# Recurrence's inverse: diagonal blocks gathered and scattered by ScalarE, transposed 64 rows at a time

## The chip, the cores and the metric

One core of a Trainium2 chip runs the whole program. The metric is the device time of one execution in microseconds; lower is better. The engines are called PE (TensorE's matmuls; PEld its weight loads), DVE (VectorE), ACT (ScalarE), POOL (GpSimd) and SP (SyncE, which issues most of the DMAs).

## What is computed

The reference is a trunk of two layers over 256 tokens of 1024 channels, in float32. In each layer three branches (latent attention with 8 heads, a spatial-gating MLP, a bidirectional RWKV-7 recurrence with 8 heads of 64) start from the same normed input, are merged by gates, and a SwiGLU follows. The part that matters here is the recurrence:

```
def step(st, inp):
    r_t, w_t, k_t, v_t, kk_t, b_t = inp
    sa = jnp.einsum('dbhij,dbhj->dbhi', st, kk_t)
    st = (st * w_t[..., None, :] - sa[..., :, None] * b_t[..., None, :]
          + v_t[..., :, None] * k_t[..., None, :])
    return st, jnp.einsum('dbhij,dbhj->dbhi', st, r_t)
```

The kernel computes it in 4 chunks of 64 tokens, for 2 directions and 8 heads: 64 systems of 64 unknowns each, whose triangular matrices have to be inverted.

## The kernel before, in words

**The threads.** The mixer of each layer is built by three generators (`interleave`): `products` (weight products for the gates, the spatial gating, the branches), `attention` and `recurrent`. Each yields the cost of what it has issued, divided by its speed (1.0, 0.5, 1.1); the thread that is behind goes next. This gives the order in which the program is written down. From it the framework's planner fixes the queue of each engine before the program runs, with costs and dependences of its own; it may put an instruction ahead of an earlier one that is not ready in its reckoning. On the chip each queue runs strictly in order.

**Weights.** A weight group arrives by DMA, ACT makes its rounded half (L347), DVE the remainder (L348), and PE uses both (L368, L380). Three to seven slots hold them, and an ACT cast waits until PE has released its slot. So every weight passes through ACT and DVE, in the same queues as the recurrence's small work.

**Recurrence.** `rw_prep` ends for each of four channel tiles with products of 64 x 64 blocks (L878) that DVE masks and writes to `MM` (L881), and PE transpositions (L884) that ACT copies out (L885). PSUM tiles of these come from a pool of two. `rw_inverse` then inverts. `MM` is laid out as [128 partitions, direction d, 32 systems u, 128 columns]: partitions 0 to 63 serve direction 0, 64 to 127 direction 1, and columns 0 to 63 hold the triangular matrix. Its 32 x 32 diagonal blocks are found at quarter q of the partitions (32 rows), d = q // 2, b = q % 2, columns 32b to 32b + 31.

- Gather (L901 to L906): for each q one DVE transposition of 32 x 1024 takes the blocks of all 32 systems out of `MM` into `Lb`, so that each of the 128 partitions then holds one system's block. It reads runs that lie 128 columns apart and changes the order of the loops on the way.
- Elimination (L907 to L914): 31 steps of two DVE operations (L910, L912) over `Lb` and `X`, which ends as the inverse of the blocks.
- L918 and L919: two transpositions of 32 x 1024 into `DN`, a copy of two of the inverted blocks in the form that the next products want.
- Scatter (L920 to L924): for each q, in the order 1, 2, 0, 3, one DVE transposition of 32 x 1024 back into `MM`.
- Two rounds of products of 32 x 32 blocks on PE put the off-diagonal blocks together. The first (L933, L934) reads `DN` and `MM`; its PSUM tiles are copied to `Wt` by ACT (L935, rows 32 to 63) and DVE (L936, rows 64 to 95). The second (L944, L945) reads `Wt` and the diagonal blocks 1 and 2 in `MM`, writes the two PSUM tiles of the same pool, and is copied to `MM` by L946 and L947.

**Attention** meets it on PE, DVE and ACT: L581 and L583 bring queries and keys into transposed form, L597 makes scores, L600 (DVE) their maxima, L603 (ACT) the exponentials, L611, L613 and L616 the transposition and the product with the values. The buffer that L583 writes shares memory with one that L884 reads.

**Memory.** `Wt` lies on columns that `rw_prep` has used for temporaries and that nothing holds between the end of `rw_prep` and L917.

Of the kernel before, what the change touches and what calls it, by code (L numbers as in the profile page):

```python
# [60 lines left out]
CI, CC, CA = 1.2, 0.8, 1.2  # L61
# [153 lines left out]
def v3(ap, b):  # L215
    return ap.rearrange("p (a b) -> p a b", b=b)
# [37 lines left out]
def trunk(ctx: ExitStack, tc: tile.TileContext, x_in, pos, wts, vecs, rows, lora, sgw, consts, out):  # L254
    nc = tc.nc
# [13 lines left out]
    ph = Phase()  # L269
# [13 lines left out]
    def pr(name="r"):  # L283
        return ps_r.tile([P, 512], F32, tag="r", name=name)
# [606 lines left out]
    def rw_inverse(MM):  # L891

        Lb = ph.get("Lb")
        X = ph.get("X")
        pt = ph.get("prod")
        nc.gpsimd.memset(X, 0.0)
        nc.gpsimd.memset(X[:, 0:1024:33], -1.0)
        MMu = MM.rearrange("p d a b c t -> p d (a b c) t")
        L3, X3 = v3(Lb, 32), v3(X, 32)
        for q in range(4):  # L900
            d, b = q // 2, q % 2  # L901
            qs = slice(32 * q, 32 * q + 32)
            src = MMu[qs, d, :, 32 * b:32 * b + 32].rearrange("p u t -> p t u")
            dst = L3[qs] if d == 0 else L3[qs].rearrange("p s t -> p t s")
            nc.vector.transpose(dst, src)  # L905
            yield 1.2 * CI  # L906
        for c in range(31):  # L907
            n, m = 31 - c, c + 1
            t = v3(pt[:, :n * m], m)
            TT(t, L3[:, c + 1:32, c:c + 1].broadcast_to([P, n, m]),  # L910
               X3[:, c:c + 1, 0:m].broadcast_to([P, n, m]), ALU.mult)
            TT(X3[:, c + 1:32, 0:m], X3[:, c + 1:32, 0:m], t, ALU.subtract)  # L912
            if c % 4 == 3:
                yield 2.0 * CI  # L914
        ph.put("prod", "Lb")
        DN = v3(ph.get("DN"), 32)
        Wt = v3(ph.get("Wt"), 32)  # L917
        nc.vector.transpose(DN[0:32].rearrange("p u s -> p s u"), X3[0:32].rearrange("p t s -> p s t"))  # L918
        nc.vector.transpose(DN[96:128].rearrange("p u s -> p s u"), X3[96:128])  # L919
        for q in (1, 2, 0, 3):  # L920
            d, b = q // 2, q % 2
            qs = slice(32 * q, 32 * q + 32)
            src = X3[qs] if d == 0 else X3[qs].rearrange("p s t -> p t s")
            nc.vector.transpose(MMu[qs, d, :, 32 * b:32 * b + 32].rearrange("p u t -> p t u"), src)  # L924
        ph.put("X")
        yield 5.0 * CI
        for hb in range(2):
            ps = pr()
            us = slice(16 * hb, 16 * hb + 16)
            for j in range(16):  # L930
                u = 16 * hb + j
                o = slice(j * 32, (j + 1) * 32)
                mm(ps[32:64, o], lhsT=MMu[0:32, 0, u, 32:64], rhs=DN[0:32, u, :], start=True, stop=True)  # L933
                mm(ps[64:96, o], lhsT=MMu[96:128, 1, u, 0:32], rhs=DN[96:128, u, :], start=True, stop=True)  # L934
            nc.scalar.copy(Wt[32:64, us, :], v3(ps[32:64, :], 32))  # L935
            nc.vector.tensor_copy(Wt[64:96, us, :], v3(ps[64:96, :], 32))  # L936
            yield 2.0 * CI
        for hb in range(2):
            ps = pr()
            us = slice(16 * hb, 16 * hb + 16)  # L940
            for j in range(16):
                u = 16 * hb + j
                o = slice(j * 32, (j + 1) * 32)
                mm(ps[0:32, o], lhsT=Wt[32:64, u, :], rhs=MMu[32:64, 0, u, 32:64], start=True, stop=True)  # L944
                mm(ps[96:128, o], lhsT=Wt[64:96, u, :], rhs=MMu[64:96, 1, u, 0:32], start=True, stop=True)  # L945
            nc.scalar.copy(MMu[0:32, 0, us, 32:64], v3(ps[0:32, :], 32))  # L946
            nc.vector.tensor_copy(MMu[96:128, 1, us, 0:32], v3(ps[96:128, :], 32))  # L947
            yield 2.0 * CI
        ph.put("DN", "Wt")
# [251 lines left out]
    for l in range(L):  # L1201
# [34 lines left out]
        def recurrent():  # L1236
            def blocks(*bs):
                while not all(("z", b) in done for b in bs):
                    yield None

            yield from blocks(12, 13, 4, 5, 6, 7)
            g2g = ph.get("g2g").rearrange("p (i c) -> p i c", i=2)
            ect = ph.get("ect").rearrange("p (n d c) -> p n d c", n=4, d=2)
            bon = ph.get("bon").rearrange("p (i h) -> p i h", i=2)
            MM = ph.at(*MIX["MM"][0]).rearrange("p (d a b c t) -> p d a b c t", d=2, a=4, b=2, c=4)
            vtok = yield from rw_prep(l, z, blocks, lo, ARF, BK, MM, ect, bon, g2g)
            done.add("p")
            yield from rw_inverse(MM)
            while "a" not in done:
                yield None  # L1250
            yield from rw_chain(l, vtok, ARF, BK, MM, ect, bon, g2g, yTc)
# [180 lines left out]
```

## Time and profile before

| | us |
|---|---|
| median of 3 runs | 1056.88 (1055.81 to 1060.32) |
| the profiled execution, its own time | 1058.36 |
| its span from first to last instruction | 1056.6 |
| busy in it: PE | 1026.2 |
| busy in it: DVE | 748.0 |
| busy in it: ACT | 548.8 |

The profile is one execution. Busy times are sums over the engine's instructions; matmuls are pipelined, and their ends are modelled, so a busy PE need not be at its peak. PEclk, or the clock, is the TensorE clock that the chip granted, as a share of full speed (2.4 GHz); 0.50 is 1.2 GHz. A "wait" is idle time of an engine, with what released it. Line numbers are those of the kernel before.

### The profile page before, as it was taken

To read this page: it belongs to the slowest core of one execution; us is meant where nothing else is said; L and a number is where in the kernel's file an instruction comes from. 1 tells how busy PE (TensorE), PEld (TensorE's weight loads), DVE (VectorE), ACT (ScalarE), POOL (GpSimd) and SP (SyncE) were. 2 spreads that over 40 slices of the span, in tenths; PEclk is the share of its full clock that TensorE was granted. 3 is DMA by queue.
4 is the path that set the end of the run, shared out by engine and by line. 5 is a ranking of instruction groups with operands and counts; after the bars stand their busy time and mean duration, and the time that the engine had idled before them with its cause. 6 is when DMAs were issued, how large, how long until landed. Compare 5 with 4: busy or idle time off the path is not lost.

```text
span 1056.6 us, 21287 instructions
## 1 busy us (share of the span) xinstructions
PE 1026.2 (97%) x8810; PEld 925.5 (88%) x8810; DVE 748.0 (71%) x1247; ACT 548.8 (52%) x903; POOL 42.0 (4%) x60
## 2 busy tenths in 40 slices
PE   9999999989999999999999999999999999999997
PEld 7987788988898899998899868889889978999885
DVE  5786899995757856664467869999857676666543
ACT  5756674644445544443366565655434465444431
POOL 2010000000200000000011000000001000000000
PEclk8999999999999999999999999999999999999999
DMA  7533441413356765653655333324215567555531
GB/s 267 190 117 101 128 143 68 140 62 112 137 180 232 274 195 187 181 181 96 208 211 185 118 109 104 122 81 140 97 48 203 200 211 264 191 186 180 180 140 40
DMA packets 46050, 164.06 MB, mean 155 GB/s; under 512 B 5233, under 2 KB 5761, under 8 KB 45954
## 3 DMA queue, kind: packets, MB, share of 16 engines
q1 hardware_dynamic: 43346, 153.90, 42.8%
q0 software_dynamic: 2464, 8.54, 2.4%
q8 instruction: 69, 1.13, 0.4%
q14 instruction: 27, 0.22, 0.1%
q10 hardware_dynamic: 144, 0.26, 0.1%
HBM read 160.59 MB, written 2.10 MB: 154 GB/s over the span
## 4 chain that ended last, share of the span: by engine, by line
PE 77%; DVE 11%; issue 4%; ACT 4%; POOL 1%; DMA 1%; SPq 0%; DVEq 0%; POOLq 0%; ACTq 0%
PE g L368 41%; PE g L380 22%; DVE permr L348 2%; DVE mix L924 1%; PE r L878 1%; PE m L616 1%; DMA permf<-in_wts_dram 1%; DVE mix L905 1%; PE m L597 1%; PE r L1036 1%; ACT mix L771 1%; PE r L815 1%; POOL yrs L409 1%; PE r L979 1%; DVE mix L824 1%
## 5 line engine op out<-in xcount | busy, mean ns | idle before, releaser
L368 PE MATMUL g<-permr 128*128 128x256 f32 x3168 | 421.3, 289 | 0.0
L368 PEld LDWEIGHTS g<-permr 128*128 128x128 f32 x3168 | 393.5, 193 | 6.4 <-issue 2.2
L348 DVE TENSOR_TENSOR permr<-permf,permr 128x1024 fp32r<-128x1024 f32 (+4 forms) x179 | 213.6, 1195 | 83.0 <-ACT permr L347 80.2
L347 ACT CAST permr<-permf 128x1024 fp32r<-128x1024 f32 (+4 forms) x179 | 183.0, 1025 | 147.0 <-PE g L368 96.5
L380 PE MATMUL g<-permr 128*128 128x512 f32 (+2 forms) x804 | 181.3, 376 | 0.0
L380 PEld LDWEIGHTS g<-permr 128*128 128x128 f32 x804 | 142.7, 190 | 24.0 <-issue 3.9
L368 PE MATMUL g<-permr,more 128*128 128x256 f32 x1008 | 121.1, 281 | 0.0
L368 PEld LDWEIGHTS g<-permr,more 128*128 128x128 f32 x1008 | 119.4, 189 | 0.0
L348 DVE TENSOR_TENSOR more<-permf,more 128x1024 fp32r<-128x1024 f32 x48 | 58.8, 1225 | 36.1 <-ACT more L347 36.0
L380 PE MATMUL g<-more,permr 128*128 128x512 f32 x324 | 79.2, 395 | 0.0
L348 DVE TENSOR_TENSOR more<-raw,more 128x1024 fp32r<-128x1024 f32 x38 | 46.5, 1225 | 43.8 <-ACT more L347 43.8
L347 ACT CAST more<-permf 128x1024 fp32r<-128x1024 f32 x48 | 50.1, 1047 | 48.7 <-PE g L368 32.5
L380 PEld LDWEIGHTS g<-more,permr 128*128 128x128 f32 x324 | 60.3, 188 | 13.7 <-DVE more L348 0.7
L347 ACT CAST more<-raw 128x1024 fp32r<-128x1024 f32 x38 | 40.0, 1051 | 51.1 <-PE g L368 23.9
L380 PE MATMUL g<-more,aT 128*128 128x512 f32 x192 | 45.5, 391 | 0.0
L380 PEld LDWEIGHTS g<-more,aT 128*128 128x128 f32 x192 | 36.0, 188 | 7.6
L348 DVE TENSOR_TENSOR permr<-raw,permr 128x1024 fp32r<-128x1024 f32 x22 | 26.9, 1224 | 21.6 <-ACT permr L347 21.6
L347 ACT CAST permr<-raw 128x1024 fp32r<-128x1024 f32 x22 | 23.0, 1044 | 26.2 <-PE g L368 12.0
L297 ACT ACTIVATE permr<-m 128x512 fp32r<-128x512 f32 (+2 forms) x36 | 19.6, 563 | 20.3 <-PE m L436 16.4
L878 PE MATMUL r<-mix,mix 64*64 64x128 f32 x512 | 28.0, 276 | 0.0
L414 ACT ACTIVATE ffn<-ffn 128x512 f32<-128x512 f32 x16 | 10.1, 630 | 33.3 <-DVE ffn L1137 33.3
L878 PEld LDWEIGHTS r<-mix,mix 64*64 64x64 f32 x512 | 21.8, 132 | 6.3 <-issue 2.9
(268 smaller groups left out, 1183.6 us busy)
## 6 DMA issues: line engine op xcount, KB each, us to landing
permf<-in_wts_dram SPq DMA_DIRECT2D x210, 512.0 KB, 4.3
raw<-in_wts_dram SPq DMA_DIRECT2D x60, 512.0 KB, 4.3
permf<-in_wts_dram SPq DMA_DIRECT2D x6, 504.0 KB, 4.8
mix<-in_rows_dram POOLq DMA_DIRECT2D x8, 256.0 KB, 3.8
ffn<-in_rows_dram POOLq DMA_DIRECT2D x4, 512.0 KB, 5.7
mix<-in_lora_dram SPq DMA_DIRECT2D x2, 768.0 KB, 7.3
permf<-in_wts_dram SPq DMA_DIRECT2D x4, 384.0 KB, 3.6
mix<-in_sgw_dram SPq DMA_DIRECT2D x2, 512.0 KB, 4.8
```

Of the source, the lines that this page charges most:

```text
L297: a = act(hi, src, AF.Copy, scale=scale)
L347: nc.scalar.copy(hi, raw)
L348: TT(lo, raw, hi.bitcast(F32), ALU.subtract)
L368: newest[0] = mm(ps, lhsT=wt[:, k, c:c + 128], rhs=xt[:, k, :], start=n == 0, stop=n == 3 * kt - 1).ins
L380: newest[0] = mm(pss[i][:, :n], lhsT=xt[:, k0 + k, i * 128:(i + 1) * 128], rhs=wt[:, k, :], start=k0 + k + q == 0, stop=q == 2 and k0 + k ...
L409: powers[:] = [nc.gpsimd.tensor_tensor(dst, src, mhalf[:, :n], ALU.pow).ins]
L597: mm(ps[:, b * 256:(b + 1) * 256], lhsT=qT[0:96, h, b * 128:(b + 1) * 128], rhs=kT[0:96, h, :], start=True, stop=True)
L616: mm(pso[:, b * 256 + h * 64:b * 256 + (h + 1) * 64], lhsT=v3(pts, 128)[:, kt * 2 + b, :], rhs=vt[:, kt, h, :], start=kt == 0, stop=kt == 1)
L771: nc.scalar.copy(dst[q * 64:(q + 1) * 64, i, :], ps[hf * 64:(hf + 1) * 64, :])
L815: mm(psd[d][hf * 64:(hf + 1) * 64, q * 256:(q + 1) * 256], lhsT=w[ds_, co:co + 64], rhs=z[ds_, 12 + q, :], start=True, stop=True)
L824: nc.vector.tensor_tensor_scan(inc, rmult, lw, 0.0, ALU.mult, ALU.add)
L878: mm(psh[hp][o, c * 128:(c + 1) * 128], lhsT=xf[hs, 4 * d + c, o], rhs=A8[hs, 4 * d + c, :], start=True, stop=True)
```

## The change

The gather is done in two steps: ACT copies the diagonal blocks of each quarter (32 rows) from `MM` into a contiguous buffer with the order of the two loops exchanged (the buffer is `Wt`, taken early and given back), and DVE transposes both quarters of a direction in one instruction of 64 rows. The scatter is done the same way backwards: one DVE transposition of 64 rows per direction into `Wt`, then two ACT copies of 32 rows into `MM`. The order of the quarters in the scatter becomes 0, 1, 2, 3. Each half of the gather yields a cost of 2.0 where each of its four quarters yielded 1.2.

```diff
--- before.py
+++ after.py
@@ -897,13 +897,16 @@
         nc.gpsimd.memset(X[:, 0:1024:33], -1.0)
         MMu = MM.rearrange("p d a b c t -> p d (a b c) t")
         L3, X3 = v3(Lb, 32), v3(X, 32)
-        for q in range(4):
-            d, b = q // 2, q % 2
-            qs = slice(32 * q, 32 * q + 32)
-            src = MMu[qs, d, :, 32 * b:32 * b + 32].rearrange("p u t -> p t u")
-            dst = L3[qs] if d == 0 else L3[qs].rearrange("p s t -> p t s")
-            nc.vector.transpose(dst, src)
-            yield 1.2 * CI
+
+        B3 = v3(ph.get("Wt"), 32)
+        for d in range(2):
+            for b in range(2):
+                qs = slice(64 * d + 32 * b, 64 * d + 32 * b + 32)
+                nc.scalar.copy(B3[qs].rearrange("p t u -> p u t"), MMu[qs, d, :, 32 * b:32 * b + 32])
+            ds = slice(64 * d, 64 * d + 64)
+            nc.vector.transpose(L3[ds] if d == 0 else L3[ds].rearrange("p s t -> p t s"), B3[ds])
+            yield 2.0 * CI
+        ph.put("Wt")
         for c in range(31):
             n, m = 31 - c, c + 1
             t = v3(pt[:, :n * m], m)
@@ -917,11 +920,12 @@
         Wt = v3(ph.get("Wt"), 32)
         nc.vector.transpose(DN[0:32].rearrange("p u s -> p s u"), X3[0:32].rearrange("p t s -> p s t"))
         nc.vector.transpose(DN[96:128].rearrange("p u s -> p s u"), X3[96:128])
-        for q in (1, 2, 0, 3):
-            d, b = q // 2, q % 2
-            qs = slice(32 * q, 32 * q + 32)
-            src = X3[qs] if d == 0 else X3[qs].rearrange("p s t -> p t s")
-            nc.vector.transpose(MMu[qs, d, :, 32 * b:32 * b + 32].rearrange("p u t -> p t u"), src)
+        for d in range(2):
+            ds = slice(64 * d, 64 * d + 64)
+            nc.vector.transpose(Wt[ds], X3[ds] if d == 0 else X3[ds].rearrange("p s t -> p t s"))
+            for b in range(2):
+                qs = slice(64 * d + 32 * b, 64 * d + 32 * b + 32)
+                nc.scalar.copy(MMu[qs, d, :, 32 * b:32 * b + 32], Wt[qs].rearrange("p t u -> p u t"))
         ph.put("X")
         yield 5.0 * CI
         for hb in range(2):
```

## Rows read from the trace of the kernel before

**Rows 1.** The page's first part: engine, busy us, share of the span, instructions.

```profile
PE 1026.2 (97%) x8810; PEld 925.5 (88%) x8810; DVE 748.0 (71%) x1247; ACT 548.8 (52%) x903; POOL 42.0 (4%) x60
```

**Rows 2.** 10-us stretches: busy us (instructions) of each engine, clock, DMA share, GB/s.

```profile
160.00:170.00 10.00, 8.88 (x92) 7.57 (x88) 9.91 (x9) 3.08 (x6) 0.00 (x0) 1.00 0.23 74
170.00:180.00 10.00, 8.95 (x67) 8.24 (x67) 9.58 (x22) 5.83 (x20) 0.00 (x0) 1.00 0.29 105
...
220.00:230.00 10.00, 7.68 (x196) 7.30 (x196) 9.90 (x7) 3.25 (x4) 1.12 (x2) 1.00 0.17 54
230.00:240.00 10.00, 10.00 (x210) 9.27 (x204) 9.81 (x15) 4.16 (x7) 0.00 (x0) 0.83 0.15 52
...
580.00:590.00 10.00, 10.00 (x72) 8.71 (x65) 9.63 (x25) 7.34 (x15) 0.00 (x0) 0.85 0.35 120
```

**Rows 3.** What TensorE waited for: us in total, times, longest us.

```profile
PE r L944 <- DVE mix L936: 4.5, 2, 2.3
...
PE m L611 <- ACT mix L603: 2.9, 2, 1.5
...
PE r L933 <- DVE mix L918: 2.0, 2, 1.0
PE r L884 <- DVE mix L881: 1.4, 2, 0.7
```

**Rows 4.** VectorE's groups by shape: busy us, mean ns of one, idle before.

```profile
L905 DVE STREAM_TRANSPOSE mix<-mix 32x1024 f32<-32x1024 f32 x8 | 16.2, 2020 | 0.2
L924 DVE STREAM_TRANSPOSE mix<-mix 32x1024 f32<-32x1024 f32 x8 | 15.8, 1980 | 0.1
...
L1038 DVE COPY mix<-r 64x512 f32<-64x512 f32 x8 | 5.6, 695 | 9.1 <-ACT mix L1037 9.0
...
L936 DVE COPY mix<-r 32x512 f32<-32x512 f32 x4 | 2.6, 683 | 0.1
```

**Rows 5.** The same view, 150 to 260 us: work over 1024 columns.

```profile
L348 DVE TENSOR_TENSOR permr<-permf,permr 128x1024 fp32r<-128x1024 f32 x17 | 20.8, 1222 | 1.0 <-ACT permr L347 0.8
L347 ACT CAST permr<-permf 128x1024 fp32r<-128x1024 f32 x17 | 17.8, 1049 | 12.7 <-PE g L368 11.3 <-PE g L380 1.1 <-DMA permf<-in_wts_dram 0.2
```

**Rows 6.** VectorE in order of time: start us, us, what; L912's first and last step.

```profile
174.68 0.21 DVE L912 TENSOR_TENSOR mix<-mix 128x31 f32<-128x31 f32 x1
...
216.37 0.19 DVE L912 TENSOR_TENSOR mix<-mix 128x31 f32<-128x31 f32 x1
```

**Rows 7.** All engines in order of time, the gather of the first layer.

```profile
161.85 1.10 PE L878 MATMUL r<-mix,mix 64*64 64x128 f32 x32
162.42 1.97 DVE L905 STREAM_TRANSPOSE mix<-mix 32x1024 f32<-32x1024 f32 x1
...
164.32 1.23 DVE L881 TENSOR_TENSOR mix<-r,permf 128x512 f32<-128x512 f32 x2
...
165.59 4.05 DVE L905 STREAM_TRANSPOSE mix<-mix 32x1024 f32<-32x1024 f32 x2
165.60 0.60 ACT L583 ACTIVATE mix<-m 96x512 f32<-96x512 f32 x1 [3.80 <-PE r L884]
...
167.34 1.03 PE L597 MATMUL m<-mix 96*128 96x256 f32 x4
...
169.67 1.29 DVE L600 TENSOR_REDUCE nm<-m 128x2 f32<-128x512 f32 x2
```

**Rows 8.** The same, the scatter of the first layer.

```profile
220.77 7.96 DVE L924 STREAM_TRANSPOSE mix<-mix 32x1024 f32<-32x1024 f32 x4
...
222.03 0.58 ACT L935 COPY mix<-r 32x512 f32<-32x512 f32 x1 [2.81 <-PE r L934]
...
223.18 4.08 PE L368 MATMUL g<-permr 128*128 128x256 f32 x32
...
229.50 0.21 PE L944 MATMUL r<-mix,mix 32*32 32x32 f32 x1 [2.25 <-DVE mix L936]
```

**Rows 9.** 1-us stretches after the scatter, columns as in rows 2.

```profile
232.00:233.00 1.00, 1.00 (x7) 1.00 (x6) 0.96 (x2) 0.84 (x2) 0.00 (x0) 0.50 0.00 0
```

## Prediction, made before the change was run

> **What bounds the kernel now.** I read the busy shares first: TensorE is busy 97% of a span of 1056.6 us, VectorE 71% [rows 1]. A change that gives TensorE no work and takes none can only win where TensorE stands still or runs below full speed, so the next view was the span in stretches of 10 us. Nearly all of them have TensorE busy for 9.4 to 10.0 us. The two stages that this change touches do not: around the gather (160 to 180 us) it is busy 8.88 and 8.95, around the scatter (220 to 230 us) 7.68, and VectorE is at 9.6 to 9.9 in all three [rows 2]. After the scatter the granted clock averages 0.83.
>
> Which wait ends last there is in the list of what TensorE waited for. Four entries, each twice (once per layer), belong to this code: L944 waits for VectorE's L936 (4.5 us in all), L611 for ScalarE's L603 (2.9), L933 for L918 (2.0), L884 for L881 (1.4) [rows 3]. Per layer that is 2.25 + 1.45 + 1.0 + 0.7 = 5.4 us; it is the prize, beside what the clock loses. VectorE's time itself is not.
>
> **What goes and what comes.** Per layer the edit takes eight transpositions of 32 rows at 2.0 us each (L905, L924: 2.02 and 1.98) and puts four of 64 rows in their place [rows 4]. A 64-row one stands nowhere in the trace. A copy of 512 columns takes 0.683 us with 32 rows and 0.695 with 64 [rows 4], so rows cost nothing on this engine, and I take 2.0. Ends: 4.0 if the two blocks of 32 were done one after the other; 1.22, the time of a tensor operation over 1024 columns [rows 5], where the new one reads and writes unbroken runs, which none of the old ones did on both sides. VectorE so loses 4 x 2.0 = 8 us per layer, 16 in all.
>
> ScalarE gets eight copies of 32 x 1024 per layer. Nearest row: its cast of 128 x 1024, 1.05 us [rows 5]. So 8.4 us per layer, 16.8 in all. ScalarE is busy 3.1 and 5.8 us of the two 10-us stretches at the gather and 3.25 of that at the scatter [rows 2]: the time is there, the order is the question. Each copy has one side with a stride of 32 elements. What a stride costs shows only in small: L912's first call of a layer walks down a column of 31 elements with that stride, its last one along 31 neighbours, and they take 0.21 and 0.19 us [rows 6]. That is 0.02 us over 31 elements, at most 0.7 us over 1024. So 1.05 is the low end, 1.05 + 0.7 = 1.75 the high one, and I take 1.05, since a rounding step of the view is half of the difference. The Trainium skill speaks against the change here: by Advanced Engine Details and Errata, section Memory Cachelines, SBUF serves lines of 16 bytes and an access that needs a new line each time pays; no figure is given. It is a rival below, priced from the rows.
>
> **Gather, per layer.** Now the first transposition (162.42 to 164.39) stands ahead of two L881 whose products TensorE finished at 162.95; they start at 164.32, and L884 waits 0.7 us for them. Then two transpositions in a row (165.59 to 169.64) stand ahead of L600, whose scores were done near 168.4; L603 and L611 wait behind it [rows 7]. After the change the first transposition waits for two copies, 2.1 us, so it can hardly start before 164. L881 then goes ahead of it, from 162.95, and L884 and L583 come up to 1.3 us earlier. The second transposition waits for two more copies and ends near 164.2 + 2.1 + 2.0 = 168.3, so L600 starts near 168.4 instead of 169.67. Gain: 0.7 + 1.3 = 2.0 us of TensorE's idle time. Against it: the second pair of copies and the two L583 (0.60 us each) [rows 7] want ScalarE at the same time. If the copies are put first, L583, on which L597, L600, L603 and L611 hang, is 2.1 us later, against 1.3 us of advance: a loss of 0.8. L583 waits for L884, and L884 for the first of the two L881; the copies wait for both L881. So the two are ready within some 0.1 us of each other, and I take the case between, one copy ahead of L583 and one behind: 2.0 - 1.05, some 0.9.
>
> The shorter yields of the gather (4.8 cost units where there were 5.76) bring the recurrence ahead of the other threads by under one unit. I price that at nothing: TensorE's queue at 180 to 210 us is full either way. If that cover fails, it is a shift of the kind that the second rival holds.
>
> **Scatter, per layer.** Now VectorE does L918, L919 and the four L924 without a break, the four from 220.77 to 228.73; L936 follows, and L944 needs the PSUM buffer that L936 empties. TensorE's last filler ends at 227.26, L944 starts at 229.50 [rows 8]. After the change: transpositions 220.77 to 222.8 and to 224.8. ScalarE's copies begin at 222.85; four by 1.05 end at 227.05. L936 overwrites rows that the third copy reads, so it waits until 226.0 and ends at 226.7. L935, on ScalarE behind the copies, ends at 227.6 (its row: 0.58 us; it now starts at 222.03 and is long done). L944 then starts at 227.65, and the idle time is 0.4 instead of 2.25: gain 1.85. So the scatter's limit moves from VectorE to ScalarE, and only 1.85 of the 4 us that VectorE saves arrive. ScalarE's casts of weights in these microseconds slip by 2 to 3 us; VectorE's backlog, busy 9.81 us of the next 10 [rows 2], stands ahead of their other halves and hides that. Without it the slip would reach TensorE. Ends: 2.25 (all of the wait) and -1.0 (copies at 1.75: 222.85 + 7.0 + 0.6 = 230.45 against 229.5).
>
> L933's wait of 1.0 us hangs on L918, the end of the chain of 31 steps, which has L348 between its steps; I book nothing, between 0 and 1.0.
>
> **Clock.** At 232 us the granted clock stands at 0.50 (1.2 GHz) with TensorE busy all the time [rows 9]. A mean of 0.83 over 10 us [rows 2] is 3.4 us at that level, 1.7 us of work lost, per layer. It has fallen by 2.5 us after the idle time before L944. If that goes, the fall may go; but the stretch 580 to 590 has a mean of 0.85 with TensorE busy for all 10 us [rows 2], so idle time is not the only thing that brings one. I book half, 0.85, between 0 and 1.7.
>
> **Sum.** Per layer 0.9 + 1.85 + 0.85 = 3.6, twice 7.2 us. The profiled execution took 1058.36 us, 1.76 more than its span, and lies 1.5 above the median of the runs, 1056.88. From it the sum gives 1051.2, at the median 1049.7. A difference under 0.5% (5.3 us) can't be told from none in measurements of this kernel.
>
> **Rivals.**
> - *All of it arrives* (0.1): both waits fully gone, L933's too, the clock stays up: 2.0 + 1.0 + 2.25 + 1.7 = 6.95 per layer, 1043.0. For it: VectorE is 4 us ahead when the 31 steps begin. Against: ScalarE's chain of four copies.
> - *Only a little arrives* (0.28): the copies take the place of the wait. On ScalarE they stand behind casts that wait for TensorE, or ahead of L583, so the gather gains nothing and the scatter 1.0 to 1.85 per layer, the clock falls as before: 1053 to 1055. For it: ScalarE's queue is in order and many of its casts wait for TensorE to free a slot; the planner that orders the queues has freedom to place the copies badly.
> - *Slower* (0.12): strided copies. One mechanism: a copy at 1.75 us or more. The scatter's chain breaks even where 222.85 + 4c + 0.6 = 229.45, at c = 1.5 us. At 1.75 it loses 1.0 per layer; in the gather the second pair holds ScalarE 1.4 us longer ahead of L583, so 0.8 + 1.4 = 2.2 lost. 3.2 per layer, 1063.3. Against it: the stride of 0.7 us in [rows 6] is an upper bound, and half of it is within the view's rounding. By the Trainium skill's rule on cachelines, cited above, this is what would come; no run here shows it for ScalarE.
> - *A 64-row transposition at 4.0 us* (0.03) would leave VectorE where it was, with the copies on top: scatter chain 228.8 + 2.1 + 0.6 = 231.5, 2.0 later, per layer: 1061. The row-count rows speak against it.
>
> **Numbers.** My forecast's case has 0.47: from 1046 (gather 2.0, clock 1.7) to 1052 (gather 0.9, no clock, 0.3 less in the scatter). Faster by over 0.5%, below 1051.6: 0.44 of this case, the 0.1 of the first rival and 0.01 of the second, 0.55. Slower, above 1062.2: 0.12 and 0.01 of the last rival, 0.13. Within 0.5%: the rest, 0.32. The range that leaves out about 2 in 10 runs from 1043.5, near the best case, to 1058.5, above the case in which little arrives.
>
> **What would show it.** Right: the new transpositions at about 2.0 us, copies at about 1.05, VectorE's busy time down by 16 us and ScalarE's up by 17; the wait before L944's products under 1 us, with ScalarE named as the one that ended it; L611's wait under 0.5 us; no stretch of clock 0.50 after the scatter. Wrong: copies at 1.5 us or more; a wait of VectorE for the copies in the gather with weight splits queued behind it and TensorE idle at 160 to 180 us as now; or an idle time that turns up later, where the group norms end.

## The result and the profile after

The change makes the kernel slower: 1070.2 us median (1066.17 to 1071.74) against 1056.79, a ratio of 1.0111, 95% interval 1.0091 to 1.0131 (the ratios here are estimated from all the runs, and are not the quotients of two medians). The profiled execution took 1070.89 us, its span is 1069.1. The page's first part (columns as in [rows 1]):

```profile
PE 1034.6 (97%) x8810; PEld 933.8 (87%) x8810; DVE 729.8 (68%) x1239; ACT 579.4 (54%) x919; POOL 42.2 (4%) x60
```

VectorE lost 18.2 us, where 16 were forecast. ScalarE got 30.6, where 17 were. So the work was moved as planned, but it is nearly twice as dear where it went. The groups by shape, ScalarE's and then VectorE's (columns as in [rows 4]), say which:

```profile
L928 ACT COPY mix<-mix 32x1024 f32<-32x1024 f32 x8 | 16.1, 2008 | 2.9 <-DVE mix L925 2.8
L905 ACT COPY mix<-mix 32x1024 f32<-32x1024 f32 x8 | 16.0, 2002 | 0.1
...
L907 DVE STREAM_TRANSPOSE mix<-mix 64x1024 f32<-64x1024 f32 x4 | 6.5, 1629 | 6.9 <-ACT mix L905 6.9
L925 DVE STREAM_TRANSPOSE mix<-mix 64x1024 f32<-64x1024 f32 x4 | 6.3, 1584 | 0.1
```

A copy took 2.00 us, not 1.05. The new transpositions average 1.6: the one of direction 0 reads and writes unbroken runs and takes 1.24, the one of direction 1 exchanges its loops and takes 2.0.

What TensorE waited for, against [rows 3] and, of the same view of before, the group norm's line, which stands first here:

```profile
PE r L1007 <- DVE mix L1002: 3.0, 4, 1.1
```

And after:

```profile
PE r L1011 <- DVE mix L1006: 5.4, 3, 1.9
PE m L611 <- ACT mix L603: 4.0, 2, 2.0
...
PE m L597 <- ACT mix L583: 2.6, 2, 1.3
PE r L948 <- DVE mix L940: 2.5, 1, 2.5
PE r L937 <- DVE mix L921: 1.9, 2, 1.0
```

L948 is the L944 of before, L937 its L933, and L1011 its L1007. L611's wait grew from 2.9 to 4.0, L597's is new, and the group norm's, at the end of the recurrence, grew by 2.4. L948's own wait did not grow in sum: 4.5 us in two before, 2.5 in one after. In the second layer it has none, since TensorE is still busy with other products, from 750 to 760 us at a clock of 0.51 in the mean. In the gather of the first layer (all engines in order of time, against [rows 7]) one sees why L597 and L611 wait:

```profile
161.24 4.07 ACT L905 COPY mix<-mix 32x1024 f32<-32x1024 f32 x2
...
165.33 0.59 ACT L583 ACTIVATE mix<-m 96x512 f32<-96x512 f32 x1
165.34 1.24 DVE L907 STREAM_TRANSPOSE mix<-mix 64x1024 f32<-64x1024 f32 x1 [1.50 <-ACT mix L905]
...
166.92 3.97 ACT L905 COPY mix<-mix 32x1024 f32<-32x1024 f32 x2
...
170.92 0.47 ACT L603 ACTIVATE mix<-m,nm 128x256 f32<-128x256 f32 x1
170.93 2.01 DVE L907 STREAM_TRANSPOSE mix<-mix 64x1024 f32<-64x1024 f32 x1 [1.94 <-ACT mix L905]
...
171.54 0.33 PE L611 MATMUL m<-permf,mix 128*128 128x128 f32 x1 [2.01 <-ACT mix L603]
```

Each pair of copies holds ScalarE for 4 us, with attention's work behind it: L583 behind the first pair, L603 (and so L611) behind the second. The scatter, against [rows 8]:

```profile
223.93 3.22 DVE L925 STREAM_TRANSPOSE mix<-mix 64x1024 f32<-64x1024 f32 x2
...
225.20 8.19 ACT L928 COPY mix<-mix 32x1024 f32<-32x1024 f32 x4 [1.40 <-DVE mix L925]
...
234.03 1.29 DVE L940 COPY mix<-r 32x512 f32<-32x512 f32 x2 [0.47 <-ACT mix L939]
...
234.77 0.21 PE L948 MATMUL r<-mix,mix 32*32 32x32 f32 x1 [2.54 <-DVE mix L940]
```

From the first transposition of the scatter to the first product of the second round it was 8.73 us (220.77 to 229.50) and is 10.84. It already starts 3.2 us late.

**Where the 12.5 us of span went.** Span less TensorE's busy time is its idle time: 30.4 us before, 34.5 after. That is 4.1 of the 12.5; the other 8.4 are busy time. The matmuls are the same 8810. What differs is the clock, a mean of 0.991 before and 0.980 after; the sum of (1 - clock) x 10 over all whole 10-us stretches is 8.5 us before and 20.6 after. (That is 12.1 more and not 8.4, since it also counts time at a low clock in which TensorE stands idle.) The stretches of after (columns as in [rows 2]):

```profile
160.00:170.00 10.00, 8.23 (x84) 7.21 (x80) 5.87 (x8) 9.17 (x8) 0.00 (x0) 1.00 0.23 74
170.00:180.00 10.00, 8.46 (x43) 8.00 (x43) 6.98 (x15) 5.75 (x16) 0.00 (x0) 0.66 0.17 52
...
750.00:760.00 10.00, 10.00 (x142) 9.94 (x137) 5.01 (x5) 9.29 (x7) 1.11 (x2) 0.51 0.29 87
```

Where before had VectorE at 9.9 and ScalarE at 3.1 (160 to 170 us), it is now 5.9 and 9.2: the bottleneck of the stage changed engines. Behind the new waits the clock fell where it had not: 170 to 180 us had 1.00 before and 0.66 after, falling to 0.50 (1.2 GHz) within the microsecond from 172, after idle times of 1.30 us before L597 and 2.01 before L611. Such a fall does not come each time: `gather_only`, below, has the same two waits and a clock of 1.00 from 160 to 180 us. In the second layer's stretch from 750 the mean is 0.51 (0.83 before).

### The profile page after: what moved, and what is told of

Its sections match the earlier page's. It is cut to its first block, busy times and chain, and to the rows that moved or that the text cites. A ratio compares the mean times of both kernels' runs of the same rounds, so it can differ in the third digit from the quotient of the medians.

```text
span 1069.1 us, 21299 instructions
## 1 busy us (share of the span) xinstructions
PE 1034.6 (97%) x8810; PEld 933.8 (87%) x8810; DVE 729.8 (68%) x1239; ACT 579.4 (54%) x919; POOL 42.2 (4%) x60
## 4 chain that ended last, share of the span: by engine, by line
PE 78%; DVE 9%; ACT 6%; issue 4%; POOL 1%; DMA 1%; POOLq 0%; DVEq 0%; ACTq 0%; SPq 0%
PE g L368 41%; PE g L380 23%; DVE permr L348 2%; PE r L878 2%; PE m L616 2%; ACT mix L905 1%; PE m L597 1%; PE r L815 1%; PE r L1040 1%; ACT mix L771 1%; PE r L380 1%; PE m L611 1%; DVE mix L824 1%; PE r L1071 1%; PE r L983 1%
## 5 line engine op out<-in xcount | busy, mean ns | idle before, releaser
L348 DVE TENSOR_TENSOR permr<-permf,permr 128x1024 fp32r<-128x1024 f32 (+4 forms) x179 | 213.1, 1193 | 81.1 <-ACT permr L347 76.5
L348 DVE TENSOR_TENSOR more<-permf,more 128x1024 fp32r<-128x1024 f32 x48 | 58.7, 1224 | 38.6 <-ACT more L347 38.6
L348 DVE TENSOR_TENSOR more<-raw,more 128x1024 fp32r<-128x1024 f32 x38 | 46.5, 1224 | 42.6 <-ACT more L347 42.5
L347 ACT CAST more<-raw 128x1024 fp32r<-128x1024 f32 x38 | 39.9, 1051 | 49.9 <-PE g L368 23.9
L348 DVE TENSOR_TENSOR permr<-raw,permr 128x1024 fp32r<-128x1024 f32 x22 | 26.9, 1224 | 21.5 <-ACT permr L347 21.5
```

Of the source, the lines that this page charges most:

```text
L347: nc.scalar.copy(hi, raw)
L348: TT(lo, raw, hi.bitcast(F32), ALU.subtract)
```

## The experiments

Theory 1: the price of ScalarE's copy, doubled by the step of 32 elements on one side, makes the change slow; the plan itself (two blocks in one transposition, copies on ScalarE) would win if the copies ran along unbroken runs. Rivals: the 64-row transposition, the place of the copies in the queues, or the changed yields. The kernel before ran again beside each group of experiments (medians 1059.34, 1059.18 and 1056.94 us), so kernels of different groups are compared by their ratios to it.

### The prices by themselves

`strides` leaves the whole computation out; it runs copies and transpositions one after another.

```python
    for eng in (lambda d, s: nc.scalar.copy(d, s), lambda d, s: nc.vector.tensor_copy(d, s), lambda d, s: nc.gpsimd.tensor_copy(d, s)):
        for s in (1, 2, 4, 8, 16):
            eng(y[0:32, :], spread(src, s))
        ...
    for r in (lo, two, slice(0, 128)):
        T(v3(y[r], 32), v3(x[r], 32))
        T(v3(y[r], 32), blocks(x, r, 32, 32))
        T(blocks(y, r, 32, 32), v3(x[r], 32))
        T(blocks(y, r, 32, 32), blocks(x, r, 32, 32))
```

> Leaves the whole computation out: single copies and transpositions of 32 x 1024 elements on each engine, with reads or writes at a step of 1, 2, 4, 8 and 16 elements, with the two loops of 32 exchanged, and in runs of 32; transpositions of 32, 64 and 128 rows with no, one or both sides exchanged. Theory 1 (the step costs): a ScalarE copy takes 1.05 us at step 1 and in runs, and 2.0 us from the step on at which each element lies in a new line of 16 bytes (4 elements), on the read side and on the write side alike; a transposition 1.2 us with neither side exchanged, 2.0 with one, whatever the number of rows. Rival (it is the engine or its neighbours in the kernel, not the step): all ScalarE copies of 32 x 1024 take the same time here, near 1.05.

ScalarE in order of time: the first line is step 1; then read and write with step 2; with step 4, the read; then the copy with two loops exchanged on the reading side; the one in runs of 32 elements on the writing side; and the exchange on the writing side. After them VectorE's four transpositions of 64 rows: no side with a step (L286), the read (L287), the write (L288), both (L289).

```profile
8.23 1.04 ACT L274 COPY y<-src 32x1024 f32<-32x1024 f32 x1 [6.22 <-DVE src L263]
15.70 1.16 ACT L274 COPY y<-src 32x1024 f32<-32x1024 f32 x1 [6.42 <-DVE src L263]
16.76 1.14 ACT L274 COPY dst<-x 32x1024 f32<-32x1024 f32 x1
17.79 2.06 ACT L274 COPY y<-src 32x1024 f32<-32x1024 f32 x1
...
28.94 1.90 ACT L274 COPY y<-x 32x1024 f32<-32x1024 f32 x1
30.75 1.04 ACT L274 COPY dst<-x 32x1024 f32<-32x1024 f32 x1
31.70 2.01 ACT L274 COPY y<-x 32x1024 f32<-32x1024 f32 x1
...
70.23 1.24 DVE L286 STREAM_TRANSPOSE y<-x 64x1024 f32<-64x1024 f32 x1
71.50 1.90 DVE L287 STREAM_TRANSPOSE y<-x 64x1024 f32<-64x1024 f32 x1
73.43 1.90 DVE L288 STREAM_TRANSPOSE y<-x 64x1024 f32<-64x1024 f32 x1
75.36 1.94 DVE L289 STREAM_TRANSPOSE y<-x 64x1024 f32<-64x1024 f32 x1
```

Theory 1 of this run holds, and its rival is out. Rows cost nothing: with 32, 64 and 128 rows the transposition with no step takes 1.23, 1.24 and 1.25 us. A step costs VectorE's transposition 0.66 us on one side and 0.70 on both, so a transposition that already has a step on one side takes a second one on the other nearly free. ScalarE's copy pays 0.9 to 1.0 for it. Runs of 32 elements cost it nothing. The price belongs to the instruction and not to the engine: VectorE's plain copies with the loops exchanged took 2.63 us each in this run. The dear step could therefore have been left where the kernel before had it.

### Each stage alone

`gather_only` has the change's first hunk alone, `scatter_only` its second.

```diff
@@ gather_only, the scatter as before @@
-            nc.vector.transpose(dst, src)
+                nc.scalar.copy(B3[qs].rearrange("p t u -> p u t"), MMu[qs, d, :, 32 * b:32 * b + 32])
...
@@ scatter_only, the gather as before @@
-            nc.vector.transpose(MMu[qs, d, :, 32 * b:32 * b + 32].rearrange("p u t -> p t u"), src)
+                nc.scalar.copy(MMu[qs, d, :, 32 * b:32 * b + 32], Wt[qs].rearrange("p t u -> p u t"))
```

> The new gather with the old scatter. Theory 1 (2.0 us copies ahead of the attention's ScalarE work): TensorE idle before L611 near 2.0 us per layer and the clock at 0.50 around 173 to 180 us, as in the changed kernel; some 3 to 5 us per layer, time 1062 to 1067. Rival (the loss sits in the scatter): 1055 to 1059.

> The old gather with the new scatter. Theory 1: four copies of 2.0 us stand ahead of L935's successor; TensorE's wait before the second round of products stays 2.3 to 2.6 us and the clock falls after it as before, so little in the scatter itself, plus what runs out later at the group norms: 1057 to 1063. Rival (the loss sits in the scatter): 1065 to 1071.

The gather alone: 1065.3 us, ratio 1.0056 (1.0036 to 1.0076). The scatter alone: 1063.8, ratio 1.0038 (1.0016 to 1.006). Together 0.94%, within the interval of the whole change; per layer about 3.0 and 2.0 us. Both stages lose, and neither makes up for the other. `gather_only` came as Theory 1 expected in its time and its waits (L597 2.6 us in two, L611 4.0), but not in the clock, which stays at 1.00 around 173 to 180 us and falls in the second layer (0.83 in the stretch from 690 us). `scatter_only` lies 0.8 us above Theory 1's range and below the rival's. Its waits before the second round of products are 0.70 and 3.23 us and not 2.3 to 2.6, 3.9 in sum where before had 4.5. TensorE's idle time grew elsewhere, from 30.4 to 34.5 us, 2.3 of it at the group norm (5.3 against 3.0), and its busy time grew by 1.6.

### The same plan with copies along unbroken runs

In `runs` ScalarE copies runs of 32 elements as they lie, and the transposition exchanges the loops on its other side too. Nothing else differs from the kernel after: on each engine the instructions stand in the same order.

```diff
-                nc.scalar.copy(B3[qs].rearrange("p t u -> p u t"), MMu[qs, d, :, 32 * b:32 * b + 32])
+                nc.scalar.copy(B3[qs], MMu[qs, d, :, 32 * b:32 * b + 32])
...
-            nc.vector.transpose(L3[ds] if d == 0 else L3[ds].rearrange("p s t -> p t s"), B3[ds])
+            nc.vector.transpose(L3[ds] if d == 0 else L3[ds].rearrange("p s t -> p t s"), B3[ds].rearrange("p u t -> p t u"))
...
-            nc.vector.transpose(Wt[ds], X3[ds] if d == 0 else X3[ds].rearrange("p s t -> p t s"))
+            nc.vector.transpose(Wt[ds].rearrange("p u t -> p t u"), X3[ds] if d == 0 else X3[ds].rearrange("p s t -> p t s"))
...
-                nc.scalar.copy(MMu[qs, d, :, 32 * b:32 * b + 32], Wt[qs].rearrange("p t u -> p u t"))
+                nc.scalar.copy(MMu[qs, d, :, 32 * b:32 * b + 32], Wt[qs])
```

> Both parts new, but the copies keep the order of the loops (runs of 32 on both sides, no step) and the transposition has the step again. Theory 1 (the step on ScalarE is the cause): copies at 1.05 us, transpositions of 64 rows at 2.0, L944's successor waits under 1 us, time 1047 to 1055. Rival (any detour over ScalarE's queue costs, the copies' length is not the point): copies at 1.05 us, but time still 1062 to 1070.

1057.17 us, ratio 0.9981 (0.9967 to 0.9996). Against the 1.0111 of the kernel after this is 1.3%, some 14 us, for the step alone: the order of the queues is no part of that difference, since it is the same. Copies (1.04 us) and transpositions (2.02 to 2.09) cost what Theory 1 expected, and the rival's 1062 to 1070 is out. But Theory 1's 1047 to 1055 us did not come either: the gain is 0.2%, 2 us. The stretches of the gather in `runs`, and then VectorE and TensorE in the scatter (L921 is the transposition that follows the elimination), with the GpSimd issue of a DMA:

```profile
160.00:170.00 10.00, 9.85 (x96) 8.91 (x96) 8.76 (x10) 8.72 (x18) 0.00 (x0) 1.00 0.24 74
170.00:180.00 10.00, 9.94 (x76) 9.02 (x75) 8.96 (x27) 5.71 (x14) 0.00 (x0) 1.00 0.35 107
...
213.40 2.08 DVE L921 STREAM_TRANSPOSE mix<-mix 32x1024 f32<-32x1024 f32 x1
...
221.37 1.13 POOL L403 DMA_DIRECT2D mix<-in_rows_dram  x2 [63.88 <-PE m L616]
...
226.31 0.69 DVE L963 TENSOR_TENSOR mix<-mix 128x512 f32<-128x512 f32 x1 [2.20 <-DMA mix<-in_rows_dram]
227.03 1.29 DVE L940 COPY mix<-r 32x512 f32<-32x512 f32 x2
...
227.77 0.21 PE L948 MATMUL r<-mix,mix 32*32 32x32 f32 x1 [1.94 <-DVE mix L940]
```

The gather's idle time is gone: TensorE is busy 19.79 of 20 us, 17.83 before [rows 2], 2.0 us more per layer (from 680 to 700 us, in the second layer, 19.80 against 17.82). The scatter still waits on VectorE's L940, 1.94 us where Theory 1 had under 1. But L940 is not late for VectorE's own work any more. Ahead of it in the queue stands L963, the recurrence's epilogue, which waits for a row of weights. Its DMA is issued at 221.37, released by L616, and L963 starts at 226.31; ScalarE's L939, for which L940 also waits, had ended at 224.87. In the kernel before L959, the same instruction, stood behind L936:

```profile
228.76 1.29 DVE L936 COPY mix<-r 32x512 f32<-32x512 f32 x2
...
231.29 0.68 DVE L959 TENSOR_TENSOR mix<-mix 128x512 f32<-128x512 f32 x1
```

### The queue behind the DMA

`runs_order` is `runs` with that block put behind the last L940 (L942 in its lines). The planner then places other instructions anew as well: 112 of VectorE's 1239 places and 956 of TensorE's 8810 hold another instruction than in `runs`. `runs_gather` is the gather of `runs` with the scatter of before. `runs_order_yield` gives back the yields' sum.

```diff
@@ runs_order against runs @@
+            inv[:] = [nc.vector.tensor_copy(Wt[64:96, us, :], v3(ps[64:96, :], 32)).ins]
...
+        with tc.issue_after(inv[0]):
             for i in range(2):
                 TT(v3(Q[:, i, :], 64), v3(vtok[:, i, :], 64), bon[:, i, :].unsqueeze(2).broadcast_to([P, 8, 64]), ALU.mult)
...
@@ runs_order_yield against runs_order @@
-            yield 2.0 * CI
+            yield 2.4 * CI
```

> As the kernel `runs` (copies in runs of 32 elements, the transposition takes the step), and besides VectorE's block of the recurrence's epilogue (the addition that waits for the DMA of its row, L963 of the kernel after) is put behind the last L940, the copy out of PSUM for which TensorE's L948 waits. Theory A (in `runs` the scatter stage gives nothing because the DMA-gated L963 stands ahead of L940: L939 was done at 224.87 us, L940 could have begun then, and it began at 227.03): the wait of L948 on L940, 1.9 us a layer, goes; with the clock's dip behind it, which costs up to 1.7 us a layer more, the time is 1050 to 1053.5 us, ratio to `before` 0.991 to 0.995. Theory B (the idle time only moves to the next wait, L937 or the group norm's L1011): within 1 us of `runs`, ratio 0.997 to 0.999, and L1011's waits grow by about what L948's lose.

> The gather stage of `runs` with the scatter stage of the kernel before (four transpositions of 32 rows, no copies). Theory A (all that `runs` gains comes from the gather stage, where TensorE's idle time went, 2.0 us a layer; its scatter stage gives nothing and moves VectorE's later work): ratio 0.995 to 0.998, as `runs` or up to 2 us better. Rival (the scatter stage of `runs` gives something of its own, and the gather's gain is lost behind it): ratio 0.999 to 1.001.

> As runs_order, with the planner told 2.4 times CI for each half of the gather stage in place of 2.0, so that the stage's whole price is that of the kernel before (4.8 times CI). Theory A (the lower price drew a few of the matmuls that fill TensorE's time away from the group norm, whose L1011 waits longer in `runs` than in `before`): its second wait on L1006 falls from about 1.9 us to under 1.2, and the time is 0.5 to 2 us under runs_order. Rival (the fillers don't matter, the group norm's chain is late for another reason): within 0.5 us of runs_order.

`runs_order`: **1049.23 us, ratio 0.9909 (0.9888 to 0.9931)**, faster than both kernels. VectorE and TensorE in its scatter, a new wait of TensorE's, and the 10 us after the scatter:

```profile
210.18 2.25 DVE L923 STREAM_TRANSPOSE mix<-mix 32x1024 f32<-32x1024 f32 x1
...
221.41 1.29 DVE L942 COPY mix<-r 32x512 f32<-32x512 f32 x2 [0.38 <-ACT mix L941]
...
222.15 0.21 PE L950 MATMUL r<-mix,mix 32*32 32x32 f32 x1 [0.26 <-DVE mix L942]
...
PE r L1054 <- ACT mix L1044: 2.9, 2, 2.0
...
230.00:240.00 10.00, 8.80 (x162) 7.72 (x162) 6.91 (x10) 5.56 (x9) 0.00 (x0) 1.00 0.41 132
```

The wait of 1.94 us is 0.26, the clock stays at 1.00 where `runs` had 0.84 in these 10 us and the kernel before 0.83. The time is Theory A's, just past the edge of its range (1049.23 us where it had 1050 to 1053.5, 0.9909 where it had 0.991 to 0.995). The DMA wait was not removed (VectorE still idles 2.12 us for it, at 231.48); it only has nothing behind it now that TensorE needs.

How the gain comes is not quite Theory A. TensorE's idle time (span less busy time) is 29.0 us in `runs` and 29.2 in `runs_order`: L948's 3.0 us became 0.5, but L1054's 2.9 are new, so the half of Theory B that says the idle time moves is right. The spans differ by 4.9 us, TensorE's busy times by 5.1. The clock averages under 0.95 in seven of the 10-us stretches from 220 to 800 us of `runs`, and in one of `runs_order`. That is not one execution's luck: the mean clock is 0.986 to 0.990 in the ten executions of `runs` and 0.994 to 0.999 in the five of `runs_order`. Nor is the DMA all that the three lines move. Two multiplications of the block (L962) and one L348 stood between the 31 steps of the elimination and no longer do, so that the steps, which begin at 170.3 us in both, take 39.9 us in place of 43.0. Of the 5.6 us by which the second round of products starts earlier (227.77 and 222.15), 3.1 are gained ahead of the scatter. How the gain divides between this, the DMA and the other new places in the queues no run shows.

The profiled span is 6.2 us under before's, 1.2 of idle and 5.0 of busy time. Some of those 5.0 lie elsewhere: the stretches from 10 and from 580 us, at 0.66 and 0.85 before, have 1.00. By the time at which TensorE ends the same weight product, they are worth 0.7 and 1.2 us. The order brings neither: `runs` has the first too, and `runs_gather` and `scatter_only` have 1.00 from 580 us. The size is therefore taken from the ratio.

`runs_gather`: 1055.6 us, 0.997 (0.9951 to 0.9989), as Theory A expected: the gather alone is worth some 3 us.

`runs_order_yield`: 1051.63 us, 0.9927 (0.9902 to 0.9953). The group norm's waits are the same 3.6 us in four, the longest 1.5, in both kernels. But TensorE's and ScalarE's queues are the same in both too, and VectorE's differs in 4 places, so the run can't tell whether fillers matter: the changed yield moved none. The median is 2.4 us over runs_order's, outside Theory A's range and its rival's 0.5, and the intervals overlap.

### Does the order do it alone?

The same three added lines, in the kernel before (`before_order`) and in the kernel after (`after_order`).

> The kernel before, with VectorE's block of the recurrence's epilogue (L959) put behind the last L936, as in runs_order, and nothing else. In the trace of the kernel before L936 already stands ahead of L959 (228.76 and 231.29 us), right behind the four transpositions. Theory A (runs_order's gain over `runs` exists only because the cheaper scatter stage leaves L940 behind a DMA; here there is nothing to take away): ratio to `before` 0.997 to 1.003. Rival (the order is worth its 7 us by itself, whatever the stages are, and could have been had without the change): ratio 0.993 or below.

> The kernel after (copies with a step of 32 elements), with the same order as runs_order; the two kernels issue the same instructions in the same order on each engine and differ only in whether the copies or the transpositions take the step. Theory A (the step's price alone makes the change slow: in the kernel after L940 waits for the four copies, which end at 233.4 us, and not for the DMA of L963, which lands at 232.9): ratio to `before` 1.008 to 1.012, within 2 us of the kernel after, and 18 to 22 us over runs_order. Rival (the order is a good part of the loss): 1.005 or below.

Before with it: 1.0013 (1.0 to 1.0026). After with it: 1.0121 (1.0101 to 1.0141), 1070.15 us, 2.1% over `runs_order` by the two ratios, some 22 us, with the instructions in the same order on every engine. Both as Theory A expected, the second just past the edge of its numbers. (The three lines shorten the elimination of the kernel after too, from 46.2 us to 41.6, so that by itself is worth nothing either.) The waits and the ScalarE and VectorE rows of `after_order`:

```profile
PE r L950 <- DVE mix L942: 6.8, 2, 3.4
...
220.47 8.18 ACT L930 COPY mix<-mix 32x1024 f32<-32x1024 f32 x4 [0.82 <-DVE mix L927]
228.67 1.06 ACT L941 COPY mix<-r 32x512 f32<-32x512 f32 x2
...
229.28 1.29 DVE L942 COPY mix<-r 32x512 f32<-32x512 f32 x2 [4.44 <-ACT mix L941]
```

With copies at 2.0 us the four of them hold the scatter's chain, and VectorE idles 4.44 us whatever stands behind L942. Of the kernels tried, the order is worth something only in the one with cheap copies.

### Copies on GpSimd

`runs_pool_order` is `runs_order` with `nc.gpsimd.tensor_copy` for the copies.

```diff
-                nc.scalar.copy(B3[qs], MMu[qs, d, :, 32 * b:32 * b + 32])
+                nc.gpsimd.tensor_copy(B3[qs], MMu[qs, d, :, 32 * b:32 * b + 32])
...
-                nc.scalar.copy(MMu[qs, d, :, 32 * b:32 * b + 32], Wt[qs])
+                nc.gpsimd.tensor_copy(MMu[qs, d, :, 32 * b:32 * b + 32], Wt[qs])
```

> As runs_order, but with the copies of both stages on GpSimd in place of ScalarE. In the micro-kernel GpSimd's copy of 32x1024 took 1.03 us, ScalarE's 1.04. Theory A (which engine copies doesn't matter so long as it is free; ScalarE's copies of PSUM, L583 and L603, then don't stand behind the gather's copies): within 1.5 us of runs_order on either side. Rival (GpSimd and VectorE hold each other up, so that copies or VectorE's own work beside them become longer): copies above 1.3 us or transpositions above 2.2 us each, and 2 us or more over runs_order.

1064.33 us, ratio 1.0047 (1.0031 to 1.0063), 15 us over `runs_order`. GpSimd's and VectorE's groups by shape, and VectorE in order of time:

```profile
L930 POOL COPY mix<-mix 32x1024 f32<-32x1024 f32 x8 | 12.0, 1504 | 100.4 <-DVE mix L927 99.9
L907 POOL COPY mix<-mix 32x1024 f32<-32x1024 f32 x8 | 11.4, 1422 | 13.2 <-DVE mix L881 13.0
...
164.33 1.94 DVE L909 STREAM_TRANSPOSE mix<-mix 64x1024 f32<-64x1024 f32 x1 [2.02 <-POOL mix L907]
166.20 1.24 DVE L881 TENSOR_TENSOR mix<-r,permf 128x512 f32<-128x512 f32 x2
...
222.34 3.20 DVE L348 TENSOR_TENSOR permr<-permf,permr 128x1024 fp32r<-128x1024 f32 x2
```

The copies take 1.42 and 1.50 us (1.03 alone), and two L348 beside them 3.20 in place of 2.36 in `runs_order`. So the rival holds: the copies are above its 1.3 us, and the loss above its 2. It does not account for 15 us: the planner also put the transposition ahead of two L881 here, as in the kernel before [rows 7], and L884 waits 1.9 us per layer for them. How the loss divides between the two was not tried.

## Why the prediction was wrong

The forecast was 1049.7 us, 7.2 faster; 1070.2 came. **The step that failed is the price of ScalarE's copy**: "I take 1.05, since a rounding step of the view is half of the difference". It measured 2.00, above even the bound of 1.75. With the step moved off the copy and every queue in the same order, the ratio is 0.9981 in place of 1.0111. Two rows were read wrongly.

- *[rows 6] was overruled though it was near the truth for its engine.* 0.02 us over 31 elements makes 0.66 us over 1024, and the micro-kernel shows a step to cost VectorE's transposition just that (1.24 to 1.90). That the two agree to the digit is luck, since with the rounding the 0.02 can be 0.01 or 0.03. I called it rounding, and where I used it as a bound I carried it to ScalarE, which pays 0.95 here (2.00 against 1.05).
- *[rows 4] and [rows 5] had the better row.* Transpositions of 1024 columns with a step took 2.0 us, VectorE's work on 1024 unbroken ones 1.22. I used the 1.22 only as an end for the new transposition, and did not ask what the difference, 0.8 us, would be once the copy had the step.

The mechanism stood in the text as the slower rival, at 0.12 and priced at 1.75 us per copy. Its own working with 2.0 gives 222.85 + 8.0 + 0.6 = 231.45 against 229.45 in the scatter, 2.0 lost, and 0.8 + 1.9 = 2.7 in the gather: 1066.3 us, 3.9 short of what came. `scatter_only` lost 2.0 per layer, `gather_only` 3.0. The Trainium skill, Advanced Engine Details and Errata, section Memory Cachelines, asks for at least two accesses to a line of 16 bytes. The micro-kernel agrees: 1.15 us at step 2 (two float32 to a line) and 2.06 at step 4 (one).

Point by point:

- *VectorE less by 16, ScalarE more by 17:* 18.2 and 30.6.
- *A 64-row transposition at 2.0 us:* 1.24 in one direction and 2.0 in the other. That rows cost nothing was right, and the 4.0 of the last rival is out.
- *Gather, a gain of 0.9:* it lost 3.0 per layer. L881 did come ahead of the transposition, as forecast (162.56 us), but the first pair of copies began at 161.24 and ended at 165.3, where two of 1.05 would have ended at 163.3, with L583 behind it. At a copy of 1.05, in `runs`, the stage gave 2.0: the full advance, where 0.9 were booked. L583 stood ahead of the whole second pair there, not between its two.
- *Scatter, a gain of 1.85:* it lost 2.0. At a copy of 1.05 the gain went to a wait that no part of my working had, the DMA ahead of L940. In `runs_order` the wait was 0.26 us, 0.4 forecast, but this agreement is luck. From the last copy's end to the second round it was 1.38 us (220.77 to 222.15) and not 0.6: the working let L936 end before L935 begins, and in the run L942 waits for L941. TensorE's queue there is another one too.
- *Clock, a gain of 0.85 per layer:* it was a loss, and the larger part of the whole: of the 12.5 us that the span grew, 8.4 are busy time. That the fall after the scatter hangs on the wait before L944 fits the first layer of `runs_order`: with the wait at 0.26 us it is gone. In the second layer the wait is as short, and a fall stays (0.83 in the stretch from 750 us).
- *L933's wait, booked at nothing:* 2.0 us before, 1.9 after. *Shorter yields, at nothing:* no run tests it. *Idle time that turns up where the group norms end*, a sign of being wrong: it came, 3.0 us before and 5.4 after.

The kernel with the prices that I assumed, copies at 1.05 and transpositions at 2.0, is `runs`, not the kernel after: 2 us under before by its ratio, where the sum said 7.2. So the price decides the sign, and with the right price the forecast would still have missed by the scatter's order. `runs_order`, which changes that order as well, is 9.6 us under; that this is near 7.2 is in part luck, since the gather gave 2.0 per layer in place of 0.9, and TensorE's busy time fell by 5.0 us in the profiled execution where 1.7 were booked for the clock.

## What to carry to other kernels

Before a strided access is moved from one engine to another, find what the step costs where it is (the same operation with and without it), and leave it with an instruction that pays for a step already; here ScalarE's copies along runs of 32 elements were free of it. When a stage gets shorter, look at what its queue now holds ahead of the next needed instruction: a wait for a DMA that was hidden behind busy work can stand bare. Compare idle and busy time apart: a kernel can win with the same idle time, at a higher clock. A wait of TensorE is not priced by its length alone: look in the stretches behind it for what the clock loses too.

## What the runs showed that was not expected

- ScalarE's copy of 32 x 1024 float32 is 1.04 us at step 1, 1.15 at step 2 and about 2.06 at step 4, on either side, and no more at 8 (2.06, 2.03) or 16 (1.89, 1.90).
- A transposition with the step on both sides costs 1.94 us, with it on one side 1.90.
- GpSimd's copies lengthened VectorE's L348, which reads two tensors in SBUF (1.64 us in the mean of the two beside them, 1.22 without), but not its transpositions (2.07 and 2.06 us). The Trainium skill, Advanced Engine Details and Errata, section Miscellaneous Facts, names VectorE's instructions with two SBUF inputs among those that conflict with GpSimd. The rows agree.
